# Layer 0 of a four-layer trunk: q's norm moved into the softmax's exponential, and the first shift weights loaded ahead of x

## The chip, the cores and the metric

One core of a Trainium2 chip runs the whole program in one launch. The metric is device time in microseconds, the median of three runs. The engines are TensorE (PE; PEld is its weight load), VectorE (DVE), ScalarE (ACT), GpSimd (POOL) and SyncE (SP), which issues nearly all transfers.

## The reference

Four layers of a diffusion transformer on 512 latent tokens and 256 context tokens of width 1024, in float32. Each layer normalizes its input, scales and shifts it by numbers made from a conditioning vector, mixes tokens (layer 0 by grouped attention) and ends with an MLP. The change lies in layer 0:

```python
def rms_norm(x, g):
    y = xf * lax.rsqrt(jnp.mean(xf * xf, axis=-1, keepdims=True) + EPS)
    return (y * g.astype(jnp.float32)).astype(x.dtype)
...
m = jax.nn.silu(vec) @ w + b          # ada_mods: shift, scale, gate, ...
hl = modulate(rms_norm(x, norm1_g[i]), ml[0], ml[1])      # h * (1.0 + scale) + shift
...
ql = apply_rope(rms_norm(ql.reshape(B, S, AT_HEADS, HEAD_DIM), q_g), ang) * scale
kl = apply_rope(rms_norm(kl.reshape(B, S, AT_KV_HEADS, HEAD_DIM), k_g), ang)
...
s = jnp.einsum('bqkgd,bnkd->bkgqn', q, k, preferred_element_type=jnp.float32)
p = jax.nn.softmax(s, axis=-1).astype(v.dtype)
```

There are 16 heads of q and 4 of k and v, each 64 wide. The norm of q is one number per token and head, so it is the same factor for a whole row of scores.

## The kernel before

Activations are held transposed, 128 channels on the partitions and tokens along the free axis. Every float32 matrix product is made of three products of a high and a low part (`mm3`, L124, L125, L127); ScalarE makes the high part and VectorE or GpSimd the low one (`split`, L104 and L105).

`start` (from L322) loads `x` in four transfers, puts the conditioning columns into rows (`sb`), and sums the squares of x: ScalarE squares one channel block (L345, L348), VectorE adds it (L349). `rstd` makes the reciprocal root, and the factor is spread over the partitions (`Rs`, L352 and L353). Scales come from VectorE's dot products of weight rows with `sb` (L223). The shift comes from TensorE: `sload(i)` loads half of its weights as four tiles `sw` (a ring of seven), `shift(i)` multiplies them with the conditioning columns (L389), ScalarE copies the row (L391), TensorE turns it into columns (L393), VectorE adds the bias (L394). There are two halves; the first is needed by the first four channel blocks. Then for each of eight blocks `modulate` makes h (VectorE L179, ScalarE L181, VectorE L182), and TensorE adds its share to k and v for three groups of 256 tokens.

`l0a` norms and rotates k, then makes q: four groups `g` of four heads, each for three token blocks `tp` (0 and 1 latent, 2 context), which gives twelve units in PSUM tiles of the role `mm` (four banks). Two units at a time go through `qk_norm` (ScalarE squares, L490; VectorE sums by head, L491; `rstd`) and `qk_unit`: VectorE multiplies by the norm (L499), GpSimd makes the sine part (L511) and VectorE the cosine part (L512), or for context the gain alone (L515); the result is split, transposed and written to DRAM (`qd`). Between the units `pump` gives VectorE dot products for the later scales. The last two units (`late`) are finished inside the attention.

`l0b` is the attention: 8 pairs of heads, 3 token blocks, 2 heads, 2 halves `u` of 128 tokens, so 96 times `front`. TensorE makes the scores into one of two PSUM tiles `s`, which take the banks of `mm` (L612); VectorE takes the negated row maximum (L614); ScalarE makes the exponential with it as its bias and sums the row (L616); TensorE transposes it (L621), ScalarE and VectorE split the copies (`pt`), and `back` multiplies with v (L635) and divides by the sums.

The order of each engine's instructions is set by the framework's scheduler, not by the code's order, except where an instruction is kept in place by `keep_in_program_order` (all loads of `load` among them).

Of the kernel before, what the change touches and what calls it, by code (L numbers as in the profile page):

```python
# [9 lines left out]
F = mybir.dt.float32  # L10
# [39 lines left out]
class Trunk:  # L50
# [78 lines left out]
    def rstd(self, ss, n, role="n", pin=False):  # L129
# [9 lines left out]
        last = ve.scalar_tensor_tensor(out=y, in0=v, scalar=1.5, in1=y, op0=ALU.add, op1=ALU.mult)  # L139
        if pin:  # L140
            self.tc.keep_in_program_order(last)
        return y
# [179 lines left out]
    def start(self):  # L322
# [4 lines left out]
        self.x = self.xp.tile([P, KC, TALL], F, name="x")  # L327
        for q in range(4):
            self.load(self.x[:, 2 * q:2 * q + 2], io["xT"][:, 2 * q:2 * q + 2])
# [5 lines left out]
        for v in range(2):  # L335
            for hf in range(2):
# [3 lines left out]
                nc.scalar.copy(out=self.sb[:, v, hf * 512:hf * 512 + 512], in_=rows)  # L340
        parts = parts_of(TALL)
# [13 lines left out]
        self.h0p = self.open("h0", "right")  # L355
        self.h = h = [self.h0p.tile([P, 2, TALL], R, name=f"h0_{j}") for j in range(KC)]
        self.kv_ps = [[self.ps("st" if w and tp == 2 else "pv" if tp == 2 else "mm") for tp in range(3)] for w in (1, 0)][::-1]
        al, ex = self.mod0
        st = self.open("start", "right")
# [18 lines left out]
        sws = {}  # L378

        def sload(i):  # L380
            for k in range(0, KC, 2):
                sws[i, k // 2] = st.tile([P, 2, 512], F, tag="sw", name="sw", bufs=7)
                self.load(sws[i, k // 2], io["ada_shift"][i][:, k:k + 2])

        def shift(i):

            rows, colv = self.ps("st"), self.ps("st")
            for k in range(KC):
                nc.tensor.matmul(rows[:2], sc[:, 2 * k:2 * k + 2], sws[i, k // 2][:, k % 2], start=(k == 0), stop=(k == KC - 1))  # L389
            r = st.tile([P, 512], F, tag="row", name="row", bufs=1)  # L390
            nc.scalar.copy(out=r[:2], in_=rows[:2])  # L391
            for n in range(4):
                nc.tensor.transpose(colv[:, 2 * n:2 * n + 2], r[:2, n * P:n * P + P], self.ident[:2, :2])  # L393
            nc.vector.tensor_tensor(out=al[:, 4 * i:4 * i + 4], in0=colv[:, :8].rearrange("p (n v) -> p n v", v=2),  # L394
                                    in1=self.vec("ada_b", 4 * i, 4 * i + 4).unsqueeze(2).to_broadcast([P, 4, 2]), op=ALU.add)

        self.share = 1 << 30
        self.pump_q = self.ada_work(0, (2, 3))
        sload(0)
# [4 lines left out]
        shift(0)  # L404
# [24 lines left out]
    def l0a(self):  # L429
# [3 lines left out]
        self.vp = kv.tile([P, 6, 4, 2, HD], R, name="vp")  # L433
        self.qd = self.dram.tile([8, P, 2, TALL], F, name="qd")
# [26 lines left out]
        for g in range(4):  # L461
            W = self.weight(io["wqkv0"][2 + g], self.wide, 256, 2)
            for tp in range(3):
# [7 lines left out]
                if len(wait) == 2 and (g, tp) != (3, 2):  # L471
                    finish()
# [885 lines left out]
```

## Time and profile before

| | us |
|---|---|
| median of 3 runs | 2752.83 |
| lowest and highest | 2746.94, 2753.98 |
| the profiled execution | 2748.76 |
| its span | 2747.0 |

Busy over the whole span: TensorE 2638.0 us (96%), VectorE 1776.1 us (65%), ScalarE 1154.8 us (42%), GpSimd 405.4 us (15%). Matrix products overlap and their ends are modelled, so TensorE's busy share says little of how near it is to its peak. These are averages over stages that differ; what follows is read stage by stage, from the span's start: `start` and the projections up to about 172 us, the hand-over, the attention up to 384 us, and all that comes behind.

### The profile page before, as it was taken

How to read it: one execution, taken by the hardware profiler on the slowest of the kernel's cores; microseconds unless marked ns; L12 is line 12 of the kernel's file. 1: busy time of each engine (PE TensorE's matmuls, PEld its weight loads, DVE VectorE, ACT ScalarE, POOL GpSimd, SP SyncE). 2: the span in 40 equal slices, each digit the busy share in tenths (PEclk: the TensorE clock that was granted, in tenths of full speed). 3: DMA queues.
4: the chain of work that ended last, by engine and by line, in shares of the span. 5: the costliest groups of instructions: out<-in, count | busy, mean ns of one | idle time of the engine just before them, and what ended most of it. 6: DMA issues, size and time to landing. Idle time of an engine off the chain costs nothing.

```text
span 2747.0 us, 39895 instructions
## 1 busy us (share of the span) xinstructions
PE 2638.0 (96%) x15472; PEld 2316.5 (84%) x15472; DVE 1776.1 (65%) x2827; ACT 1154.8 (42%) x2052; POOL 405.4 (15%) x359
## 2 busy tenths in 40 slices
PE   7989899999999999998999999998999998999998
PEld 5878778888888888988988889888888887988888
DVE  7988879766453372268766657998666657644445
ACT  3458864212121342268523335656322245533323
POOL 2321212000000030034200004543000012200002
PEclk8999999999999999999999999999999999999999
DMA  7431234445442256488466644213466633333334
GB/s 269 133 123 36 77 120 147 139 145 153 137 140 85 77 168 209 138 201 190 161 206 207 190 147 139 77 47 107 133 212 200 206 124 107 123 115 94 98 100 123
DMA packets 124844, 384.85 MB, mean 140 GB/s; under 512 B 17264, under 2 KB 37872, under 8 KB 123632
## 3 DMA queue, kind: packets, MB, share of 16 engines
q1 hardware_dynamic: 121392, 379.17, 44.2%
q10 hardware_dynamic: 3264, 3.15, 0.3%
q8 instruction: 122, 2.00, 0.3%
q14 instruction: 66, 0.54, 0.1%
HBM read 354.98 MB, written 27.26 MB: 139 GB/s over the span
## 4 chain that ended last, share of the span: by engine, by line
PE 49%; DVE 4%; DMA 2%; ACT 1%; issue 0%; POOL 0%; DVEq 0%; SPq 0%; ACTq 0%; POOLq 0%
PE ps_mm L124 15%; PE ps_mm L125 15%; PE ps_mm L127 15%; DVE ps_st L1162 1%; DMA k<-k 1%; DMA q<-q 1%; PE ps_cv L124 1%; PE ps_cv L125 1%; PE ps_cv L127 1%; DVE h L182 0%; PE ps_s L881 0%; PE ps_pt L890 0%; PE ps_cv L995 0%; PE ps_cv L998 0%; PE ps_cv L999 0%
## 5 line engine op out<-in xcount | busy, mean ns | idle before, releaser
L104 ACT CAST wh<-raw 128x1024 fp32r<-128x1024 f32 (+1 forms) x397 | 419.6, 1060 | 1030.6 <-PE ps_mm L125 606.5
L105 DVE TENSOR_TENSOR wl<-raw,wh 128x1024 fp32r<-128x1024 f32 (+1 forms) x368 | 463.7, 1262 | 372.6 <-ACT wh L104 369.5
L194 POOL TENSOR_TENSOR S<-S,tmp_q 128x256 f32<-128x256 f32 (+1 forms) x104 | 144.8, 1392 | 1684.8 <-ACT tmp_q L193 1680.7
L124 PE MATMUL ps_mm<-u,wh 128*128 128x512 f32 (+1 forms) x1088 | 374.9, 346 | 0.0
L125 PE MATMUL ps_mm<-u,wh 128*128 128x512 f32 (+1 forms) x1088 | 373.8, 345 | 0.0
L127 PE MATMUL ps_mm<-u,wl 128*128 128x512 f32 (+1 forms) x1088 | 373.6, 346 | 0.0
L125 PE MATMUL ps_mm<-hm,wh 128*128 128x512 f32 (+1 forms) x912 | 331.2, 365 | 0.0
L127 PE MATMUL ps_mm<-hm,wl 128*128 128x512 f32 (+1 forms) x912 | 331.0, 365 | 0.0
L124 PE MATMUL ps_mm<-hm,wh 128*128 128x512 f32 (+1 forms) x912 | 328.2, 366 | 1.1 <-ACT hm L181 1.1
L223 DVE CUSTOM_DVE_ANT_0 prod<-araw,sb 128x1024 bf16<-128x1024 f32 x224 | 276.4, 1234 | 6.5 <-DMA araw<-in_ada 5.3
L206 DVE SCALAR_TENSOR_TENSOR x<-ps_mm,mod,x 128x256 f32<-128x256 f32 (+1 forms) x192 | 115.1, 605 | 246.8 <-PE ps_mm L127 241.1
L125 PEld LDWEIGHTS ps_mm<-u,wh 128*128 128x128 f32 x1088 | 206.1, 189 | 25.0
L127 PEld LDWEIGHTS ps_mm<-u,wl 128*128 128x128 f32 x1088 | 205.9, 189 | 25.2
L124 PEld LDWEIGHTS ps_mm<-u,wh 128*128 128x128 f32 x1088 | 205.7, 189 | 25.3 <-DVE x L206 0.4
L127 PEld LDWEIGHTS ps_mm<-hm,wl 128*128 128x128 f32 x912 | 172.6, 189 | 27.6 <-DVE wl L105 0.4
L125 PEld LDWEIGHTS ps_mm<-hm,wh 128*128 128x128 f32 x912 | 172.7, 190 | 27.2
L124 PEld LDWEIGHTS ps_mm<-hm,wh 128*128 128x128 f32 x912 | 170.8, 190 | 28.7 <-ACT hm L181 1.5
L104 ACT CAST u<-tmp_r 128x512 fp32r<-128x512 f32 (+2 forms) x143 | 89.0, 624 | 171.1 <-DVE tmp_r L738 170.9
L124 PE MATMUL ps_big<-hm,wh 128*128 128x512 f32 x464 | 157.4, 339 | 0.8 <-ACT wh L104 0.8
L105 DVE TENSOR_TENSOR u<-tmp_r,u 128x512 fp32r<-128x512 f32 (+2 forms) x143 | 99.1, 695 | 86.6 <-ACT u L104 86.2
L125 PE MATMUL ps_big<-hm,wh 128*128 128x512 f32 x464 | 145.9, 337 | 0.0
L124 PE MATMUL ps_mm<-wh,h 128*128 128x256 f32 x448 | 129.9, 291 | 7.3 <-DVE tmp_r L499 2.9
(311 smaller groups left out, 5781.6 us busy)
## 6 DMA issues: line engine op xcount, KB each, us to landing
raw<-in_w SPq DMA_DIRECT2D x288, 512.0 KB, 3.9
araw<-in_ada SPq DMA_DIRECT2D x176, 512.0 KB, 3.7
raw<-in_wo SPq DMA_DIRECT2D x32, 512.0 KB, 4.3
raw<-in_wpw SPq DMA_DIRECT2D x24, 512.0 KB, 3.5
raw<-in_wqk SPq DMA_DIRECT2D x16, 512.0 KB, 4.1
q<-q SPq DMA_DIRECT2D x32, 256.0 KB, 9.1
raw<-in_wft SPq DMA_DIRECT2D x16, 512.0 KB, 3.8
k<-k SPq DMA_DIRECT2D x32, 224.0 KB, 9.4
```

Source lines behind the costliest of these rows:

```text
L104: self.nc.scalar.copy(out=H, in_=src)
L105: (low or self.nc.vector).tensor_tensor(out=L, in0=src, in1=H.bitcast(F), op=ALU.subtract)
L124: mm(o, lhs[0], rh, start=(k == 0), stop=False)
L125: mm(o, lhs[0], rl, start=False, stop=False)
L127: mm(o, lhs[1], rh, start=False, stop=last)
L194: (add or nc.gpsimd).tensor_tensor(out=S[:, :w], in0=S[:, :w], in1=q, op=ALU.add)
L206: self.nc.vector.scalar_tensor_tensor(out=xm, in0=self.like(ps), scalar=gate[:, m:m + 1], in1=xm, op0=ALU.mult, op1=ALU.add)
L223: ins = self.nc.vector.tensor_tensor_reduce(out=junk, in0=t, in1=self.sb[:, v], op0=ALU.mult, op1=ALU.add, scale=1.0, scalar=0.0, accum_ou ...
L1162: keep(nc.vector.scalar_tensor_tensor(out=y if last else a, in0=ut, scalar=wt, in1=a, op0=ALU.mult, op1=ALU.add))
```

## The change

**The start.** The first half of the shift's weights is loaded ahead of x, and its products, row copy and columns are written ahead of the sum of squares. The second half stays where it was.

```diff
         self.x = self.xp.tile([P, KC, TALL], F, name="x")
+        self.h0p = self.open("h0", "right")
+        st = self.open("start", "right")
...
+        sload(0)
         for q in range(4):
             self.load(self.x[:, 2 * q:2 * q + 2], io["xT"][:, 2 * q:2 * q + 2])
...
                 nc.scalar.copy(out=self.sb[:, v, hf * 512:hf * 512 + 512], in_=rows)
...
+        shift(0)
         parts = parts_of(TALL)
...
         self.pump_q = self.ada_work(0, (2, 3))
-        sload(0)
         for j in range(2):
             mods(j)
             wload(j)
         sload(1)
-        shift(0)
```

**The norm of q.** `squares` replaces the first half of `qk_norm`. A unit of q is no longer multiplied by its norm: for latent tokens ScalarE copies it out of PSUM for GpSimd, and VectorE's cosine product reads PSUM; for context the gain product reads PSUM. Units go through one at a time, and the norm is made once for the three units of a group, into `rsq`. In the attention the negated maximum is multiplied by the norm's column, and the exponential takes that column as its scale. k is treated as before, its three squares being summed by `squares` too.

```diff
+        self.rsq = kv.tile([P, 4, 24], F, name="rsq")
...
-            for a, r in zip(wait, self.qk_norm([a[0] for a in wait])):
-                self.qk_unit(a[0], r, a[1], 0, a[2], wk, tab, qkg)
+            for ps, tp, g in wait:
+                if tp == 0:
+                    sums[g] = self.small(24, "h")
+                self.squares(ps, sums[g], tp)
+                self.qk_unit(ps, None, tp, 0, g, wk, tab, qkg)
+                if tp == 2:
+                    self.rstd(sums[g], HD, "h", out=self.rsq[:, g])
                 self.pump(1)
...
-                if len(wait) == 2 and (g, tp) != (3, 2):
+                if g < 3 or tp == 0:
                     finish()
...
-        qn = self.tmp("r")
-        nc.vector.tensor_tensor(out=qn.rearrange("p (n d) -> p n d", d=HD), in0=ps.rearrange("p (n d) -> p n d", d=HD),
-                                in1=rs.unsqueeze(2).to_broadcast([P, 8, HD]), op=ALU.mult)
+        if rs is not None:
+            qn = self.tmp("r")
+            nc.vector.tensor_tensor(out=qn.rearrange("p (n d) -> p n d", d=HD), in0=ps.rearrange("p (n d) -> p n d", d=HD),
+                                    in1=rs.unsqueeze(2).to_broadcast([P, 8, HD]), op=ALU.mult)
+        elif tp < 2:
+            qn = self.tmp("r")
+            nc.scalar.copy(out=qn[:, :512], in_=ps)
+        else:
+            qn = ps
+        qn = qn[:, :512]
...
-            nc.vector.tensor_tensor(out=o4, in0=q4, in1=tab[:, a, 0, 2 * tp:2 * tp + 2].unsqueeze(2).to_broadcast([P, 2, 4, HD]), op=ALU.mult)
+            c4 = q4 if rs is not None else ps.rearrange("p (t h d) -> p t h d", t=2, h=4)
+            nc.vector.tensor_tensor(out=o4, in0=c4, in1=tab[:, a, 0, 2 * tp:2 * tp + 2].unsqueeze(2).to_broadcast([P, 2, 4, HD]), op=ALU.mult)
...
             nc.vector.tensor_reduce(out=mx, in_=ps[:, kc:TALL], axis=AX.X, op=ALU.max, negate=True)
+            n = part * 8 + u * 4 + pair % 2 * 2 + hh
+            rs = self.rsq[:, pair // 2, n:n + 1]
+            nc.vector.tensor_tensor(out=mx, in0=mx, in1=rs, op=ALU.mult)
             p = wk.tile([P, TALL], F, tag="p", name="p", bufs=3)
-            nc.scalar.activation(p[:, kc:], ps[:, kc:TALL], AF.Exp, bias=mx, accum_out=sums[:, u, hh:hh + 1])
+            nc.scalar.activation(p[:, kc:], ps[:, kc:TALL], AF.Exp, bias=mx, scale=rs, accum_out=sums[:, u, hh:hh + 1])
```

The scheduler lays the instructions out anew. Line numbers in the order of the change are its own; `small`, `tmp` and `mod` are the norm's columns, the work tiles and the scales and shifts. TensorE at the start, before (L339 the conditioning rows, L155 and L148 the sum over channels and its spread, L389 and L393 the shift, L124 the first products):

```order
L339 MATMUL ps_st<-ident,scol 128x128 x16
L155 MATMUL ps_st<-ones,tmp_r 128x1 x6
L148 MATMUL ps_st<-ident,small_ny 128x128 x6
L389 MATMUL ps_st<-sw,scol 2x512 x8
L393 MATMUL ps_st<-ident,row 128x2 x4
L124 MATMUL ps_mm<-wh,h_0_187 128x256
```

and in the changed kernel:

```order
L350 MATMUL ps_st<-ident,scol 128x128 x16
L358 MATMUL ps_st<-sw,scol 2x512 x8
L362 MATMUL ps_st<-ident,row 128x2 x4
L156 MATMUL ps_st<-ones,tmp_r 128x1 x6
L149 MATMUL ps_st<-ident,small_ny 128x128 x6
L124 MATMUL ps_mm<-wh,h_0_215 128x256
```

VectorE at the same place, before (L349 the additions of squares, L135 to L137 the norm's chain):

```order
L334 TENSOR_TENSOR scol<-scol,vecs 128x16
L349 TENSOR_TENSOR tmp_r<-tmp_r,araw 128x768 x7
L135 TENSOR_SCALAR small_nv<-ps_st 128x6
L136 RECIPROCAL small_ny<-small_nr 128x6
L137 TENSOR_TENSOR small_nv<-small_nv,small_ny 128x6
```

and in the changed kernel:

```order
L345 TENSOR_TENSOR scol<-scol,vecs 128x16
L375 TENSOR_TENSOR tmp_r<-tmp_r,araw 128x768 x3
L363 TENSOR_TENSOR mod_69<-ps_st,vecs 128x8
L375 TENSOR_TENSOR tmp_r<-tmp_r,araw 128x768 x4
L135 TENSOR_SCALAR small_nv<-ps_st 128x6
```

The shift's products and columns have moved ahead of the sum over channels on TensorE, and its bias addition (L394, now L363) to between the third and the fourth addition of squares on VectorE, where before it stood just ahead of the first low part of h (L182).

VectorE at the end of the projections, before, from the last sums of squares (L491) to the first maximum (L614):

```order
L491 TENSOR_REDUCE small_h<-tmp_q 128x8
L105 TENSOR_TENSOR pk<-S,pk 128x8x64 x2
L491 TENSOR_REDUCE small_h<-tmp_q 128x8
L135 TENSOR_SCALAR small_hv<-small_h 128x16
L136 RECIPROCAL small_hy<-small_hr 128x16
L137 TENSOR_TENSOR small_hv<-small_hv,small_hy 128x16
L138 TENSOR_TENSOR small_hv<-small_hv,small_hy 128x16
L139 SCALAR_TENSOR_TENSOR small_hy<-small_hv,small_hy 128x16
L499 TENSOR_TENSOR tmp_r<-ps_mm,small_hy 128x512 x2
L512 TENSOR_TENSOR S<-tmp_r,tab 128x512
L515 TENSOR_TENSOR S<-tmp_r,qkg 128x512
L614 TENSOR_REDUCE small_m<-ps_s 128x1 x2
```

and in the changed kernel, where L498 is the sum, L526 and L529 the table products, L628 the maximum and L631 the new multiplication:

```order
L498 TENSOR_REDUCE small_h<-tmp_q 128x8
L526 TENSOR_TENSOR S<-ps_mm,tab 128x512
L105 TENSOR_TENSOR pk<-S,pk 128x8x64
L498 TENSOR_REDUCE small_h<-tmp_q 128x8
L529 TENSOR_TENSOR S<-ps_mm,qkg 128x512
L135 TENSOR_SCALAR small_hv<-small_h 128x24
L136 RECIPROCAL small_hy<-small_hr 128x24
L137 TENSOR_TENSOR small_hv<-small_hv,small_hy 128x24
L138 TENSOR_TENSOR small_hv<-small_hv,small_hy 128x24
L105 TENSOR_TENSOR pk<-S,pk 128x8x64
L140 SCALAR_TENSOR_TENSOR rsq<-small_hv,small_hy 128x24
L628 TENSOR_REDUCE small_m<-ps_s 128x1 x2
```

The table products stand directly behind the sums of squares and read PSUM; the norm's chain (L135 to L140) comes behind them.

VectorE within the attention, before, a stretch of one pair of heads (L614 maximum, L105 low part of the transposed exponential, L568 fold, L555 and L557 the reciprocal of the row sums):

```order
L614 TENSOR_REDUCE small_m<-ps_s 128x1
L105 TENSOR_TENSOR pt_3578<-ps_st,pt_3577 128x384
L614 TENSOR_REDUCE small_m<-ps_s 128x1
L105 TENSOR_TENSOR pt_3578<-ps_st,pt_3577 128x384
L105 TENSOR_TENSOR pt_3636<-ps_st,pt_3635 128x256
L555 RECIPROCAL rs<-sums 128x4
L557 COPY tmp_q<-rs 128x256
L105 TENSOR_TENSOR pt_3636<-ps_st,pt_3635 128x256
L614 TENSOR_REDUCE small_m<-ps_s 128x1
L568 TENSOR_TENSOR tmp_t<-ps_pv,tmp_t 64x256
L614 TENSOR_REDUCE small_m<-ps_s 128x1
L568 TENSOR_TENSOR tmp_t<-ps_pv,tmp_t 64x256
```

and in the changed kernel (L628 maximum, L631 the new multiplication, L582 fold):

```order
L628 TENSOR_REDUCE small_m<-ps_s 128x1
L105 TENSOR_TENSOR pt_3403<-ps_st,pt_3402 128x384
L631 TENSOR_TENSOR small_m<-small_m,rsq 128x1
L582 TENSOR_TENSOR tmp_t<-ps_pv,tmp_t 64x256
L105 TENSOR_TENSOR pt_3403<-ps_st,pt_3402 128x384 x2
L628 TENSOR_REDUCE small_m<-ps_s 128x1
L631 TENSOR_TENSOR small_m<-small_m,rsq 128x1
L105 TENSOR_TENSOR pt_3470<-ps_st,pt_3469 128x384
L628 TENSOR_REDUCE small_m<-ps_s 128x1
L569 RECIPROCAL rs<-sums 128x4
L631 TENSOR_TENSOR small_m<-small_m,rsq 128x1
L571 COPY tmp_q<-rs 128x256
```

Some of the multiplications stand directly behind their maximum, others one or more instructions later. On SyncE's queue, behind the attention, two loads of scale weights (`araw`) have also moved ahead of the second load of x.

## Rows read from the trace of the kernel before

**Rows 1.** Stages of layer 0: busy us by engine, granted clock, DMA.
```profile
core 0: us, PE busy (x) PEld busy (x) DVE busy (x) ACT busy (x) POOL busy (x), PEclk, DMA share, GB/s
34.00:84.00 50.00, 45.60 (x314) 38.28 (x315) 48.78 (x89) 19.94 (x36) 9.53 (x10) 0.95 0.49 169
84.00:172.00 88.00, 83.60 (x665) 82.28 (x665) 86.18 (x144) 35.18 (x62) 33.91 (x26) 0.95 0.49 162
172.00:185.00 13.00, 6.72 (x45) 5.74 (x44) 7.90 (x15) 5.72 (x10) 5.17 (x5) 0.87 0.25 81
185.00:384.00 199.00, 179.40 (x1269) 158.77 (x1270) 172.06 (x351) 172.86 (x453) 37.74 (x47) 0.97 0.14 46
```

**Rows 2.** VectorE's timeline: start, us, instruction [idle before, releaser].
```profile
9.80 6.27 DVE L349 TENSOR_TENSOR tmp_r<-tmp_r,araw 128x768 f32<-128x768 f32 x6 [1.24 <-ACT araw L348]
...
33.42 0.17 DVE L394 TENSOR_TENSOR mod<-ps_st,vecs 128x8 f32<-128x8 f32 x1 [4.86 <-PE ps_st L393]
34.38 1.15 DVE L182 SCALAR_TENSOR_TENSOR h<-tmp_t,mod,h 128x512 fp32r<-128x512 f32 x2 [0.79 <-ACT h L181]
```

**Rows 3.** Timelines of TensorE and ScalarE, the shift's products and the cast.
```profile
22.54 8.01 PE L389 MATMUL ps_st<-sw,scol 128*2 128x512 f32 x16
...
31.48 0.40 ACT L375 CAST wh<-raw 128x256 fp32r<-128x256 f32 x1 [7.79 <-DMA raw<-in_wqkv]
```

**Rows 4.** X's transfers (first and last issue), SyncE's timeline.
```profile
L100 SPq DMA_DIRECT2D x<-in_xT x4: 417/428/477, 1.2 to 2.6; - x4
DMA to landing us min/median/max: 4.7/6.9/9.0
...
15.44 10.32 SPq L100 DMA_DIRECT2D sw<-in_ada_shift  x4
```

**Rows 5.** Stretches of the start, columns as in rows 1.
```profile
8.00:10.00 2.00, 0.00 (x0) 0.00 (x0) 0.77 (x2) 2.00 (x5) 0.00 (x0) 1.00 1.02 427
...
22.00:24.00 2.00, 2.00 (x5) 0.42 (x4) 1.89 (x6) 1.47 (x4) 0.53 (x1) 0.50 0.94 373
26.00:28.00 2.00, 2.00 (x6) 0.42 (x5) 2.00 (x4) 0.00 (x0) 0.00 (x0) 1.00 0.68 209
```

**Rows 6.** Lines L499 and L512 (ns min/median/max), and VectorE's timeline of one norm.
```profile
L499 DVE TENSOR_TENSOR tmp_r<-ps_mm,small_hy x14: 679/682/692, 94.3 to 180.6; 128x512 f32<-128x512 f32 x14
...
L512 DVE TENSOR_TENSOR S<-tmp_r,tab x10: 680/1220/1234, 96.9 to 181.2; 128x512 f32<-128x512 f32 x10
...
167.43 0.17 DVE L135 TENSOR_SCALAR small_hv<-small_h 128x16 f32<-128x16 f32 x1
...
168.41 1.29 DVE L499 TENSOR_TENSOR tmp_r<-ps_mm,small_hy 128x512 f32<-128x512 f32 x2
```

**Rows 7.** Timelines of ScalarE, TensorE and VectorE at the hand-over to attention.
```profile
176.03 0.60 ACT L490 ACTIVATE tmp_q<-ps_mm 128x512 f32<-128x512 f32 x1 [0.62 <-PE ps_mm L127]
...
180.78 2.29 PE L612 MATMUL ps_s<-kd,q 128*128 128x512 f32 x8 [4.35 <-DVE tmp_r L499]
...
183.16 1.81 DVE L614 TENSOR_REDUCE small_m<-ps_s 128x1 f32<-128x768 f32 x2
```

**Rows 8.** Two pairs of heads (columns as in rows 1); VectorE's timeline.
```profile
251.44:275.11 23.67, 21.84 (x159) 19.34 (x159) 21.40 (x45) 21.05 (x57) 4.44 (x6) 1.00 0.10 34
...
322.41:350.18 27.77, 24.31 (x158) 21.79 (x159) 22.93 (x46) 23.21 (x56) 9.05 (x8) 0.88 0.42 143
...
252.81 0.17 DVE L555 RECIPROCAL rs<-sums 128x4 f32<-128x4 f32 x1
252.90 0.53 DVE L105 TENSOR_TENSOR pt<-ps_st,pt 128x384 fp32r<-128x384 f32 x1
...
256.89 0.18 DVE L555 RECIPROCAL rs<-sums 128x4 f32<-128x4 f32 x1
257.10 0.29 DVE L557 COPY tmp_q<-rs 128x256 f32<-128x256 f32 x1
```

**Rows 9.** VectorE's timeline behind attention.
```profile
391.88 0.75 DVE L206 SCALAR_TENSOR_TENSOR x<-ps_mm,mod,x 128x512 f32<-128x512 f32 x1 [5.50 <-DMA x<-in_xT]
```

More of the change, by code (lines that the diff above doesn't have):

```diff
@@ L327, in start, with sload @@
         self.x = self.xp.tile([P, KC, TALL], F, name="x")
+        self.h0p = self.open("h0", "right")
+        st = self.open("start", "right")
+        sws = {}
+        def sload(i):
+            for k in range(0, KC, 2):
+                sws[i, k // 2] = st.tile([P, 2, 512], F, tag="sw", name="sw", bufs=7)
+                self.load(sws[i, k // 2], io["ada_shift"][i][:, k:k + 2])
+        sload(0)
         for q in range(4):
@@ L340, in start, with shift @@
                 nc.scalar.copy(out=self.sb[:, v, hf * 512:hf * 512 + 512], in_=rows)
+        al, ex = self.mod0
+        def shift(i):
+            rows, colv = self.ps("st"), self.ps("st")
+            for k in range(KC):
+                nc.tensor.matmul(rows[:2], sc[:, 2 * k:2 * k + 2], sws[i, k // 2][:, k % 2], start=(k == 0), stop=(k == KC - 1))
+            r = st.tile([P, 512], F, tag="row", name="row", bufs=1)
+            nc.scalar.copy(out=r[:2], in_=rows[:2])
+            for n in range(4):
+                nc.tensor.transpose(colv[:, 2 * n:2 * n + 2], r[:2, n * P:n * P + P], self.ident[:2, :2])
+            nc.vector.tensor_tensor(out=al[:, 4 * i:4 * i + 4], in0=colv[:, :8].rearrange("p (n v) -> p n v", v=2),
+                                    in1=self.vec("ada_b", 4 * i, 4 * i + 4).unsqueeze(2).to_broadcast([P, 4, 2]), op=ALU.add)
+        shift(0)
         parts = parts_of(TALL)
@@ L376, in wload @@
                 nc.gpsimd.tensor_tensor(out=L[:, j], in0=raw[:, j], in1=H[:, j].bitcast(F), op=ALU.subtract)
[L378 to L395, printed above, removed]
         self.share = 1 << 30
         self.pump_q = self.ada_work(0, (2, 3))
-        sload(0)
         for j in range(2):
@@ L448, in l0a @@
             self.split(pv, *(self.vp[:, 2 * tp:2 * tp + 2, :, s] for s in range(2)))
[L449 removed]
+        ss = self.small(24, "h")
         for tp in range(3):
[L451 removed]
+            self.squares(self.kv_ps[0][tp], ss, tp)
+        rs = self.rstd(ss, HD, "h")
+        for tp in range(3):
+            self.qk_unit(self.kv_ps[0][tp], rs[:, 8 * tp:8 * tp + 8], tp, 1, 0, wk, tab, qkg)
             self.pump(1)
[L453 removed]
+        wait, sums = [], {}
         def finish():
[L456 to L457 removed]
+            for ps, tp, g in wait:
[5 more added lines that the diff above has]
+                    self.rstd(sums[g], HD, "h", out=self.rsq[:, g])
                 self.pump(1)
```

27 lines of the change are left out of this document (8 added, 19 removed).

## The prediction

> **What bounds the kernel now.** The change touches only layer 0, so I first cut its span into stages and read each engine's busy time there [rows 1]. From 34 to 172 us, in the front projections, VectorE is the bound: 48.78 of 50 us and then 86.18 of 88 us busy, with TensorE behind it. From 172 to 185 us, where projections give way to attention, nobody works much: 6.72 us of TensorE and 7.90 us of VectorE in 13. From 185 to 384 us, in attention, three engines are close together: TensorE 179.40, ScalarE 172.86 and VectorE 172.06 us of 199. So one microsecond of VectorE is worth about one microsecond before 172 us, nothing by itself in the hand-over, and something between nothing and one in attention. After 384 us only a few instructions change places.
>
> Second, the waits at the start. VectorE finishes the sum of squares at 16.07 us (9.80 + 6.27), and later stands still for 4.86 us until the shift is there (L394, at 33.42 us) and for 0.79 us until L182 [rows 2]. The shift is late because TensorE runs its products only from 22.54 to 30.55 us, and ScalarE, which must copy their row, stands in a cast that waits 7.79 us for a weight load [rows 3]. That load was held by SyncE: the second set of shift weights occupies its queue for 10.32 us, since the seven `sw` buffers are not free before the first products are done [rows 4].
>
> **The change, part by part.** *A, the start.* The four shift transfers (2.1 MB) now stand ahead of x in SyncE's queue. The last part of x was issued at 2.6 us and landed 9.0 us later, at 11.6 us [rows 4]; at 427 GB/s [rows 5] 2.1 MB take 4.9 us, so it lands near 16.5. The order adds a second thread: L394 stands between the third and the fourth of the seven additions, and behind it come four at 1.05 us each (6.27 / 6). TensorE's shift products (eight, in the trace sixteen instructions) take 8.01 us where part of them ran at half clock [rows 3]; they can start when the transposes ahead of them end near 8 us, so they end near 15 to 16 us, copy and column transposes end near 16.3 us, and four additions later the sum is there at 20.4 us. The transfer's own bound (16.5 us plus three steps, 19.6 us) is close to it. The sum is 4.3 us later than 16.07 us. From there to where VectorE now falls idle, at 28.56 us (33.42 - 4.86), the work is the same, so that point comes at 32.9 us; but the shift is there, and L182 follows at once instead of at 34.38 us. Gain: 1.5 us, not the 5.65 us that the two waits show. Bounds: if the sum is only 2 us late, 3.8 us are gained. If the products run wholly at half clock (the granted clock was 0.50 from 22 to 24 us after TensorE had been idle, 1.00 from 26 to 28 us [rows 5]), they last nearly 14 us, the sum is near 26.5 us and 5 us are lost. I take the first, since TensorE comes to these products from the transposes, at granted clock 1.00 still at 8 to 10 us. SyncE's 10.32 us vanish as well, but the loads that were behind them have no waiter left that sets the end.
>
> *B, projections up to 172 us.* For q the multiplication by the norm (L499) falls away: 12 instructions, ten of them before 172 us, at 0.6 us from start to start (1.29 us for two, less their overlap) [rows 6]: 6.0 us. The norm's chain of six instructions ran for each pair of units, six times; now once for each group, four times. Back to back its VectorE part took 0.98 us (167.43 to 168.41 us) [rows 6], threaded between other work about half; two fewer are 1 us. Added is a ScalarE copy for eight units, 0.6 us each like the square of the same tile [rows 7]: 4.8 us on an engine with 35.18 of 88 us busy [rows 1], hidden. VectorE is the bound, so the gain is 7 us. Bounds: TensorE has only 4.4 us of gaps there (88 - 83.60), so 4 us if its busy time is real work; and 11 us, if the eight L512 that now read PSUM run like L499, whose 14 never took over 0.692 us, and not at their median of 1.22 us [rows 6] (8 x 0.54 = 4.3 us).
>
> *C, the hand-over.* The last unit's square starts at 176.03 us, but the scores' first product waits until 180.78 us, 4.35 us of it on L499, which had to wait for the norm; the first maximum starts at 183.16 us [rows 7]. By the new order the scores' PSUM is free after square, copy and the two table multiplications, none of which needs the norm: about 1.9 us after 176.03 us, so near 178 us. The first maximum comes near 179.5 us, the first exponential behind two maxima and two new multiplications. I take 3 us, between 2 and 4.5.
>
> *D, attention.* 96 multiplications of 128x1 are added on VectorE, between each maximum and its exponential. No row shows one; the nearest is the reciprocal of 128x4. With an independent instruction behind it, it costs 0.09 us from start to start (252.81 to 252.90 us), with a dependent one 0.21 us (256.89 to 257.10 us) [rows 8]. In the new order 30 of the 96 stand right behind their maximum and 66 have one to four instructions between. The first kind I price at 0.22 us, the second at 0.09 us: 6.6 + 5.9 = 12.5 us of VectorE. A pair of heads takes 23.67 us, of which VectorE is busy 21.40 us [rows 8]. The idle 2.27 us could absorb it; but in the pair from 322.41 us, into which three weight splits fall, the period grew to 27.77 us although VectorE stood idle for 4.84 us of it [rows 8]: in this stage added work lengthens the period while every engine still has gaps. I let a fifth be absorbed: loss 10 us, period 24.9 us. Bounds: 2 us, if VectorE's gaps take nearly all; 20.2 us, if each costs 0.21 us and nothing is absorbed. ScalarE's exponential takes its scale from a column; as with its bias column I count nothing for that.
>
> By a rule of the Trainium skill ("VectorE: DVE Perf Modes", The DRAIN you can't avoid) the next VectorE instruction does not start until the pipe is empty, semaphore or not. The row of 0.17 us with the next start after 0.09 us does not agree. By the rule every one of the 96 would cost its full length wherever it stands, and the sum would be the first rival's, +8.7 us.
>
> *E, behind attention.* SyncE's order puts two transfers of 512 KB ahead of x's second load, for which VectorE waits 5.50 us at 391.88 us [rows 9]. They are 2.5 us at 427 GB/s, but VectorE can work on them meanwhile. Nothing, 2 us either way.
>
> The sum: -1.5 - 7 - 3 + 10 + 0 = **-1.5 us**, against the profiled execution's 2748.76 us: 2747.3 us. The median of the runs shown lies 4.1 us higher, at 2752.83 us, and would become 2751.3 us. I state 2750 us, between the two.
>
> **The rivals.** *Attention pays in full (slower).* The multiplication sits where three engines are tied together: two score buffers are held from product to exponential, and two thirds of the multiplications wait behind another VectorE instruction, so the exponential comes later, ScalarE's queue with it, then TensorE's transposes. At 0.21 us each and nothing absorbed attention loses 20.2 us: 20.2 - 11.5 = +8.7 us, 2761.5 us on the median, and up to 2767 us with the delay on top. It decides when a pair takes over 26.2 us (8 x 2.5 = 20). For it: the gaps did not absorb the weight splits. Against: 66 of 96 cost less than half of that by the row. Chance 0.19.
>
> *Attention absorbs it (faster).* VectorE's gaps take the small instructions; D is 2 us, the sum -9.5 us, and with L512 faster too -13.8 us: 2743 to 2739 us. It decides when a pair takes under 24.1 us. For it: 2.27 us idle against 1.6 us added in a pair; against it the same pair from 322.41 us. Chance 0.24.
>
> *The start turns round.* The change puts x behind the shift, and the norm behind both: if the products run at half clock, the sum ends near 26.5 us and the early shift does not do what it is there for. A becomes +5 us, the sum +5 us: 2758 us, inside what can be told from no change. Chance 0.07.
>
> **How the numbers follow.** The forecast case (a pair of 24.1 to 26.2 us, sum between -8 and +8 us) has 0.50. Within 0.3%, which is 8.3 us and about what a measurement of this kernel can tell from no change, lie the forecast and the turned start: 0.57. Faster by more: 0.24; slower by more: 0.19. The bounds added up reach from about -20 to +21 us, which would need every term at its end; leaving out 2 in 10 gives -16 to +13 us on the median: 2737 to 2766 us.
>
> **What would show it.** In the profile of the changed kernel L394 should start near 16 us, the last addition end near 20.4 us, and L182 follow without a wait near 33 us; the end of the projections should come 8 to 9 us earlier, the first score product about 11 us earlier, near 170 us; a pair of heads should take 24.9 us, with the small multiplications at 0.17 us each. Wrong would be: additions that end after 24 us; projections no shorter, with TensorE or ScalarE busy all through; or a pair under 24.1 or over 26.2 us.

## The result and the profile after

The changed kernel takes **2787.2 us** (median of four runs, 2785.8 to 2789.5) against 2749.9 us of the kernel before beside it: a ratio of **1.0136, 95% interval 1.0116 to 1.0156**. It is 37 us slower; the forecast was 2750 us, with a range up to 2766 us.

The profiled execution spans 2784.0 us, 37.0 us more than before. Cut at three places it shows where they are:

| | before | after | difference |
|---|---|---|---|
| first score product of attention starts | 180.78 | 177.04 | -3.7 |
| from there to the first product of `wo0` | 203.6 | 243.5 | **+39.9** |
| from there to the end of the span | 2362.6 | 2363.4 | +0.8 |

The loss is in attention and nowhere else (`wo0` is the attention's output weight, whose products come right behind it). The stages, with the columns of [rows 1], which they answer:

```profile
34.00:84.00 50.00, 43.74 (x305) 36.64 (x304) 48.90 (x91) 18.42 (x32) 8.83 (x9) 0.94 0.49 168
84.00:168.00 84.00, 77.27 (x621) 75.73 (x620) 77.50 (x120) 37.53 (x67) 37.45 (x27) 0.96 0.50 169
168.00:181.00 13.00, 10.84 (x86) 10.28 (x84) 5.72 (x13) 4.96 (x10) 2.78 (x4) 1.00 0.23 81
181.00:421.00 240.00, 190.39 (x1274) 164.70 (x1275) 188.83 (x447) 187.95 (x454) 39.50 (x48) 0.96 0.12 40
```

In attention VectorE works 16.8 us and ScalarE 15.1 us more than in the last line of [rows 1], in a stage that is 41 us longer; no engine is busy for more than 80% of it, where three were at 86 to 90%. So no engine has become the bound; the engines wait for each other. One pair of heads of the steady part, after (it answers the first line of [rows 8]):

```profile
262.76:289.90 27.14, 22.61 (x158) 19.71 (x158) 23.92 (x57) 22.75 (x57) 4.44 (x6) 1.00 0.08 30
```

27.14 us against 23.67, at a granted TensorE clock of 1.00 in both: VectorE is idle for 3.2 us of it, ScalarE for 4.4, TensorE for 4.5. Whom TensorE waits for in attention stands in its list of waits (us in total, times, the longest), here the first line of before and the first two of after:

```profile
PE ps_st L621 <- ACT p L616: 6.2, 12, 2.1
```

```profile
PE ps_st L638 <- ACT p L633: 29.2, 31, 5.0
PE ps_pv L652 <- DVE pt L105: 10.3, 18, 1.5
```

The transposes of the probabilities (L621, now L638) stand in TensorE's queue and wait for the exponential 29.2 us instead of 6.2; what is behind them in the queue waits too. And the exponential waits for the new multiplication. ScalarE's first and third wait in attention before, then its first two after:

```profile
ACT pt L104 <- PE ps_st L621: 14.3, 22, 2.1
...
ACT p L616 <- DVE small_m L614: 4.1, 2, 3.8
```

```profile
ACT pt L104 <- PE ps_st L638: 22.7, 37, 1.4
ACT p L633 <- DVE small_m L631: 18.0, 34, 1.5
```

One front (product, maximum, multiplication, exponential) of the steady part, from the timeline of all engines (start, us, engine and line, operation):

```profile
301.13 0.94 DVE L628 TENSOR_REDUCE small_m<-ps_s 128x1 f32<-128x768 f32 x1
...
302.00 0.55 DVE L105 TENSOR_TENSOR pt<-ps_st,pt 128x384 fp32r<-128x384 f32 x1
...
302.46 0.15 DVE L631 TENSOR_TENSOR small_m<-small_m,rsq 128x1 f32<-128x1 f32 x1
...
303.11 1.01 ACT L633 ACTIVATE p<-ps_s,small_m,rsq 128x768 f32<-128x768 f32 x1
```

The maximum ends at 302.07. VectorE then does a low part of the front before (L105), and only at 302.46 the multiplication, whose own 0.15 us are the smallest item; meanwhile, at 302.37, ScalarE has begun two casts of transposes (L104), and the exponential starts 1.04 us behind the maximum. I call this stretch, from the end of a maximum to the start of its exponential, the **gap**. Taken over all 96 fronts (nth maximum with nth exponential) its mean is 0.68 us before and 1.35 us after: 0.70 us until the multiplication starts, 0.25 us for it, 0.40 us from its end to the exponential.

### The profile page after: what moved, and what is told of

The parts are those of the page before. It is cut to its first block, busy times and chain, and to the rows that moved or that the text cites. A ratio compares the mean times of both kernels' runs of the same rounds, so it can differ in the third digit from the quotient of the medians.

```text
span 2784.0 us, 40011 instructions
## 1 busy us (share of the span) xinstructions
PE 2649.4 (95%) x15472; PEld 2324.6 (83%) x15472; DVE 1782.3 (64%) x2901; ACT 1171.9 (42%) x2058; POOL 408.2 (15%) x359
## 4 chain that ended last, share of the span: by engine, by line
PE 78%; DVE 11%; DMA 5%; ACT 3%; issue 2%; POOL 0%; SPq 0%; DVEq 0%; ACTq 0%; POOLq 0%
PE ps_mm L124 18%; PE ps_mm L125 18%; PE ps_mm L127 18%; PE ps_big L124 6%; PE ps_big L127 6%; PE ps_big L125 6%; DMA k<-k 2%; DVE small_m L628 2%; DVE pt L105 2%; ACT p L633 1%; DVE prod L224 1%; DVE ps_st L1179 1%; DMA qd<-qs 1%; PE ps_pv L652 1%; PE ps_st L638 1%
## 5 line engine op out<-in xcount | busy, mean ns | idle before, releaser
L104 ACT CAST wh<-raw 128x1024 fp32r<-128x1024 f32 (+1 forms) x397 | 419.5, 1060 | 1036.2 <-PE ps_mm L125 601.7
L105 DVE TENSOR_TENSOR wl<-raw,wh 128x1024 fp32r<-128x1024 f32 (+1 forms) x368 | 465.0, 1265 | 376.1 <-ACT wh L104 373.4
L124 PE MATMUL ps_mm<-u,wh 128*128 128x512 f32 (+1 forms) x1088 | 374.9, 346 | 0.0
L124 PE MATMUL ps_mm<-hm,wh 128*128 128x512 f32 (+1 forms) x912 | 328.2, 366 | 1.1 <-ACT hm L182 1.1
L124 PEld LDWEIGHTS ps_mm<-u,wh 128*128 128x128 f32 x1088 | 205.7, 189 | 25.6 <-DVE x L207 0.4
L125 PEld LDWEIGHTS ps_mm<-u,wh 128*128 128x128 f32 x1088 | 206.1, 189 | 24.9
L125 PEld LDWEIGHTS ps_mm<-hm,wh 128*128 128x128 f32 x912 | 172.7, 190 | 27.1
L124 PEld LDWEIGHTS ps_mm<-hm,wh 128*128 128x128 f32 x912 | 170.8, 190 | 28.9 <-ACT hm L182 1.5
L104 ACT CAST u<-tmp_r 128x512 fp32r<-128x512 f32 (+2 forms) x143 | 89.0, 624 | 170.6 <-DVE tmp_r L755 170.3
L124 PE MATMUL ps_big<-hm,wh 128*128 128x512 f32 x464 | 157.4, 339 | 0.8 <-ACT wh L104 0.8
L105 DVE TENSOR_TENSOR u<-tmp_r,u 128x512 fp32r<-128x512 f32 (+2 forms) x143 | 99.0, 695 | 86.5 <-ACT u L104 86.2
L124 PE MATMUL ps_mm<-wh,h 128*128 128x256 f32 x448 | 130.1, 292 | 7.6 <-ACT h L182 4.6
```

The costliest lines, as they stand in the source:

```text
L104: self.nc.scalar.copy(out=H, in_=src)
L105: (low or self.nc.vector).tensor_tensor(out=L, in0=src, in1=H.bitcast(F), op=ALU.subtract)
L124: mm(o, lhs[0], rh, start=(k == 0), stop=False)
L125: mm(o, lhs[0], rl, start=False, stop=False)
```

## The experiments

First I took the change apart. Theory A1: the multiplication costs it; A2: the exponential's scale column; B: neither, but the new order of the work.

**no_factor**, the attention as before, the rest as changed:

```diff
-            nc.vector.tensor_tensor(out=mx, in0=mx, in1=rs, op=ALU.mult)
-            nc.scalar.activation(..., AF.Exp, bias=mx, scale=rs, ...)
+            nc.scalar.activation(..., AF.Exp, bias=mx, ...)
```

> The changed kernel with the factor taken out of the attention: no multiplication of the maximum, no scale column in the exponential; q stays without its norm (this part of the computation is left out). Theory A (the two additions in the attention cost all of it): the pair period goes back to 23.7 us, attention to about 204 us, and the time to 2746 us (2749.9 less the 3.7 us that the changed kernel has gained by the first score product). Theory B (the new order of the work from the projections on costs it, not the additions): the period stays over 26 us and the time over 2770 us.

Measured: 2750.9 us, 1.0002 (0.9993 to 1.0012); a pair takes 23.66 us, attention 206.1 us. With the factor out all of the loss is gone, so B falls, as far as the new order does not itself come from the factor. But the 3.7 us ahead of attention did not reach the median either.

**mult_only**, factor and scale as `self.one`, a column of ones; the exponential without `scale`:

```diff
+            nc.vector.tensor_tensor(out=mx, in0=mx, in1=self.one, op=ALU.mult)
+            nc.scalar.activation(..., AF.Exp, bias=mx, ...)
```

> The changed kernel with the multiplication of the maximum kept, by a column of ones, and the exponential without a scale column (q's norm is left out of the computation). Theory A1 (the multiplication in the chain from maximum to exponential carries most, 0.25 us on VectorE and a place further back in its queue): period about 26.5 us, time 2770 to 2783 us. Theory A2 (the exponential that is 0.09 us longer with a column carries most): period about 24 us, time below 2755 us.

Measured: 2803.3 us, 1.0192 (1.0176 to 1.0207), attention 253.9 us, gap 1.52 us. In attention the multiplication alone costs more than the whole change, 47.8 us over no_factor, and twice its own 23 us: a sum of durations does not give it. Its pairs are uneven, 26.7 to 33.2 us, where those of the changed kernel settle at 27.1; why it is slower than the whole change isn't settled.

**scale_only**, `scale=self.one` in the exponential, no multiplication:

> The changed kernel with a scale column of ones in the exponential and no multiplication of the maximum (q's norm is left out of the computation). Theory A1: 96 exponentials longer by 0.09 us, 8.6 us on ScalarE, a part of them hidden: 2750 to 2755 us, the rest of the loss gone with the multiplication. Theory A2: 2775 us or more. If each alone costs little (both below 2757 us), it is the two together that fill the slack of the loop.

Measured: 2753.4 us, 1.0011 (1.0001 to 1.0021), attention 207.9 us. The column costs its time on ScalarE, but hardly anything at the end. Line L630 of no_factor and L633 of this run (min/median/max ns):

```profile
L630 ACT ACTIVATE p<-ps_s,small_m x96: 474/902/943, 181.8 to 378.6; 128x768 f32<-128x768 f32 x64, 128x256 f32<-128x256 f32 x32
```

```profile
L633 ACT ACTIVATE p<-ps_s,small_m,one x96: 571/996/1027, 182.4 to 381.7; 128x768 f32<-128x768 f32 x64, 128x256 f32<-128x256 f32 x32
```

**start_only**, the shift's loads and products ahead of x, q's norm where it was:

> The kernel before with the first part of the change alone: the shift's weights and products ahead of x, q's norm where it was. Theory (the start gains, the attention loses): the 3.5 us by which the first part of h comes earlier in the changed kernel reach the end whole, 2746 us, and the pair period stays at 23.7 us. Rival (the projections take it back, since TensorE waits there for other work): 2749 to 2750 us.

Measured: 2758.9 us, 1.003 (1.002 to 1.004): neither. The first low part of h comes at 31.17 us, 3.2 us earlier than before, but the first score product only 0.6 us earlier (180.21), attention takes 208.4 us, and 6 us more than before pass behind it. There, from the first product of `wo0` to the end, the kernels run here differ by -5 to +11 us from the kernel before (2357.8 to 2373.6 us), in steps of some 2 to 4 us in layers that none of them edits. Why isn't settled; so below attention itself is compared, cut out of the trace, beside the time.

**q_only**, the second part of the change alone:

> The second part of the change alone: q's norm in the exponential's factor, the shift's weights where they were before. Theory (the attention loses and the start brings the 3.5 us that the trace of the changed kernel shows): 2788 to 2793 us, first score product near 180 us, period about 27 us. Rival (the two parts do harm only together, as the start moves the projections' work against the loads): below 2775 us.

Measured: 2785.8 us, 1.014 (1.0123 to 1.0157), period 27.13 us, gap 1.35 us. It is the whole loss. Its first score product starts at 175.51 us, earlier than with both parts together (177.04): the start's gain does not add to this one.

So it is the multiplication. Next: what about it? Q: its place behind other work in VectorE's queue; L: its collisions with GpSimd; T: VectorE's time as such.

**ts_mult**, the same multiplication with the factor as a per-row scalar:

```diff
-            nc.vector.tensor_tensor(out=mx, in0=mx, in1=rs, op=ALU.mult)
+            nc.vector.tensor_scalar(out=mx, in0=mx, scalar1=rs, scalar2=None, op0=ALU.mult)
```

> The changed kernel with the multiplication of the maximum written as tensor by per-row scalar, so that VectorE reads one tensor from SBUF and the factor as a scalar, not two tensors. In the changed kernel 28 multiplications that met a GpSimd operation took 0.49 us on average and ended with it, 65 that met none took 0.15 us. Theory L (an operation on two SBUF tensors can't run beside GpSimd's): all 96 take about 0.15 us, VectorE gains some 9 us, time about 2775 us. Rival (the place in the queue and the step in the chain cost it, not these 9 us): time within 4 us of 2787 us, whatever the durations do.

Measured: 2776.0 us, 1.0096 (1.0079 to 1.0113). The line of the multiplication in the changed kernel, then in this run:

```profile
L631 DVE TENSOR_TENSOR small_m<-small_m,rsq x96: 139/149/742, 182.3 to 417.8; 128x1 f32<-128x1 f32 x96
```

```profile
L631 DVE TENSOR_SCALAR small_m<-small_m,rsq x96: 183/205/217, 187.3 to 412.0; 128x1 f32<-128x1 f32 x96
```

The scalar form is slower in the median but never longer than 0.22 us, whether GpSimd runs or not. L's forecast of some 2775 us held, 11 of the 37 us, though not its 0.15 us: VectorE saved 3.9 us on the multiplications, and the gap fell to 1.15 us.

**act_mult**, the multiplication on ScalarE right ahead of its exponential:

```diff
+            nc.scalar.activation(mx, mx, AF.Copy, scale=rs)
```

> The changed kernel with the multiplication of the maximum on ScalarE, right ahead of its exponential, instead of on VectorE. VectorE's queue is then that of the kernel before, ScalarE has 96 operations more of about 0.2 us, 19 us in all. Theory Q (the multiplication's place behind other work in VectorE's queue holds the exponentials back): the waits of the exponentials shrink, period 24.5 to 25.5 us, 2760 to 2768 us. Rival (any operation more between maximum and exponential costs its own time on the loop, 0.2 us twelve times and more): period over 26 us, 2775 us or more.

Measured: 2779.5 us, 1.0112 (1.0096 to 1.0129); one takes 0.30 us, not 0.2; period 26.66 us, gap 1.11 us. Q's forecast is missed and its rival's (over 26 us, 2775 us or more) met: out of VectorE's queue it costs nearly as much. ScalarE is now busy 24.80 of 26.66 us, so this run mixes a longer gap with a fuller engine.

**pool_mult**, on GpSimd:

```diff
+            nc.gpsimd.tensor_tensor(out=mx, in0=mx, in1=rs, op=ALU.mult)
```

> The changed kernel with the multiplication of the maximum on GpSimd, which is busy for 39.5 of the attention's 240 us. Theory B (VectorE's busy time is what the loop lacks): VectorE has its old work, period about 24 us, 2755 us. Rival (the length of the chain from maximum to exponential is what counts): the way over GpSimd adds its latency and, at times, 0.74 us of an operation in front, period over 27 us, 2785 us or more.

Measured: 2763.7 us, 1.0055 (1.004 to 1.007); period 24.68 us, gap 0.76 us. Here the multiplication starts 0.13 us behind its maximum, since GpSimd is mostly free. The forecasts (2755 us for VectorE's relief, which is T, and 2785 us or more for the chain) are both missed, and two readings fit: VectorE is relieved (T), or the gap is short.

**fused_ts**, maximum and factor in one pass over the scores, written to p (`rs` holds the negated factor):

```diff
-            nc.vector.tensor_reduce(out=mx, in_=ps[:, kc:TALL], axis=AX.X, op=ALU.max, negate=True)
-            nc.vector.tensor_tensor(out=mx, in0=mx, in1=rs, op=ALU.mult)
+            nc.vector.tensor_scalar(out=p[:, kc:], in0=ps[:, kc:TALL], scalar1=rs, scalar2=3.0e38,
+                                    op0=ALU.mult, op1=ALU.min, accum_out=mx)
+            nc.scalar.activation(p[:, kc:], p[:, kc:], AF.Exp, bias=mx, scale=-1.0, ...)
```

> The changed kernel with maximum and multiplication in one pass of VectorE: scores times the negated factor from PSUM into p, with the smallest of the row as the accumulated result; the exponential then reads p from SBUF with a scale of -1 and that bias, without a scale column; four more operations of 128x24 negate the factor ahead of the attention. No operation of its own is left for the factor but a read of the accumulator (0.08 us at L902 of the changed kernel). Theory (the separate multiplication costs it): the pass takes about the 0.95 us of the maximum, the exponential about as long as now, period 23.7 to 24.5 us, time 2746 to 2758 us. Rival (the pass that writes 128x768 is longer or stands in GpSimd's way): a pass of 1.2 us or more, period over 26 us, 2770 us or more.

Measured: 2755.4 us, 1.0024 (1.0014 to 1.0033), gap 0.48 us, a pair in 24.2 to 24.3 us. The wide pass takes 1.01 us and its accumulator read 0.08, together 0.14 more than the maximum's 0.95; 32 us of the loss are gone:

```profile
L632 DVE TENSOR_SCALAR_CACHE_REDUCE p<-ps_s,rsq 128x768 f32<-128x768 f32 x64 | 64.7, 1012 | 7.5 <-PE ps_st L638 5.7 <-PE ps_s L627 0.9
...
L632 DVE DVE_READ_ACCUMULATOR p<-ps_s,rsq 128x1 f32 x96 | 7.9, 83 | 0.0
```

I then held T for the likelier theory, and three runs were to show it.

**off_chain**, no factor, but a multiplication whose result nobody reads:

```diff
+            nc.vector.tensor_tensor(out=self.small(1, "j"), in0=mx, in1=self.one, op=ALU.mult)
```

> The changed kernel without the factor (q's norm is left out of the computation), but with 96 multiplications of the maximum by a column of ones on VectorE whose result nobody reads: the same queue time as in the run that kept the multiplication alone, but no exponential waits for it. Theory T (VectorE's time is what the loop lacks; that run lost 52 us by 23 us of operations): most of the loss stays, 2775 us or more, period over 26 us. Rival (the step in the chain from maximum to exponential, and where it stands in the queue, costs it): time below 2760 us, period below 24.5 us.

Measured: 2759.7 us, 1.0042 (1.0027 to 1.0057); attention 204.8 us, gap 0.60 us; what is lost in time lies behind attention (2373.6 us, 11 more than before). **T falls.** The same 96 operations are in VectorE's queue as in mult_only (18 and 23 us), but no exponential waits for them, and attention is 49 us shorter. Attention of off_chain, then of mult_only:

```profile
177.00:382.00 205.00, 179.42 (x1284) 159.83 (x1283) 186.07 (x455) 176.78 (x456) 37.91 (x47) 0.98 0.13 45
```

```profile
178.00:432.00 254.00, 203.44 (x1283) 171.10 (x1282) 193.04 (x455) 182.90 (x456) 38.56 (x48) 0.95 0.11 36
```

VectorE, here the busiest engine, does its 186 us in 205 without harm. It had the room; what the loop had not was time between maximum and exponential.

**before_copy** and **fused_copy**, the 24 copies of the reciprocals (0.29 us each on VectorE, 0.40 on GpSimd) moved to GpSimd, in the kernel before and in fused_ts:

```diff
-        nc.vector.tensor_copy(out=re.rearrange(
+        (nc.gpsimd if w == 256 else nc.vector).tensor_copy(out=re.rearrange(
```

> The kernel before with the 24 copies of the reciprocals over 128x256 (L557, 0.29 us each, 6.9 us) on GpSimd, which is idle for 160 of the attention's 199 us. Theory T (what VectorE's queue holds goes whole into the loop): the period falls by up to 0.9 us (3 copies of 0.29) to 22.8 to 23.3 us and the time by 3 to 7 us, to 2743 to 2746 us, faster than both kernels. Rival (TensorE, at 21.84 of 23.67 us, and the chain decide): period 23.6 us, time within 2 us of the kernel before.

> The one-pass form of maximum and factor with the 24 copies of the reciprocals on GpSimd as well. The one-pass form took 2755.4 us at a mean pair period of some 24.3 us, VectorE's pass and accumulator read being 0.15 us longer than the maximum. Theory T: 7 us less on VectorE give back 3 to 7 us, 2748 to 2752 us, level with the kernel before. Rival (its loop is bound by TensorE's wait for the score buffers): 2755 us, unchanged.

Measured: before_copy 2751.9 us, 1.0014 (1.0005 to 1.0023), period 23.81 us: relief of VectorE brings nothing, against T once more. fused_copy 2748.5 us, 1.000 (0.999 to 1.0009): its gain of 7 us over fused_ts is what T gave as a number, but it is no proof of T: in the profiled executions 3.0 us are gained in attention (210.4 to 207.4 us, a pair in 24.0 us) and 8.1 us behind it, in layers that neither edits, while 2.9 us are lost ahead of it. It is the best form of the change, 39 us faster than the changed kernel. Level with the kernel before it is only by the part behind attention (4.8 us shorter); its attention is 3.8 us longer. No run beat both kernels.

Left open was whether the gap itself is the cause, since each kernel with a longer gap had also put work on VectorE or ScalarE. The last two runs lengthen it on GpSimd alone:

**pool_x2, pool_x4**, behind pool_mult's multiplication one and three more by ones:

```diff
             nc.gpsimd.tensor_tensor(out=mx, in0=mx, in1=rs, op=ALU.mult)
+            nc.gpsimd.tensor_tensor(out=mx, in0=mx, in1=self.one, op=ALU.mult)
```

> The multiplication of the maximum on GpSimd, followed there by one more by a column of ones: one operation of 0.19 us more in the chain from maximum to exponential, on an engine that is idle for most of the attention. With one operation the time was 2763.7 us, attention 216.1 us, and the maximum's end lay 0.76 us ahead of the exponential's start on average. Theory C (the length of this chain sets the loop; over the runs so far some 0.55 us of attention per front for each us of it): gap about 1.0 us, attention about 226 us, time about 2774 us. Rival Q (the queue time on VectorE or ScalarE sets it): no more work there, 2762 to 2766 us.

> The same with three operations by ones behind the multiplication on GpSimd, 0.57 us more in the chain and none on VectorE or ScalarE. Theory C: gap about 1.35 us, as in the changed kernel, attention 240 to 250 us, time about 2790 us. Rival Q: 2762 to 2770 us. If GpSimd itself became the bound (58 us more on 39.5 and 19 us in some 230 us), its share would show it; at half of the time it is not.

Measured: 2780.5 us, 1.0104 (1.0081 to 1.0127), gap 1.15, attention 229.7 us; and 2799.1 us, 1.0175 (1.0155 to 1.0194), gap 1.56, attention 255.4 us. Theory C holds in both, at more than its numbers. Attention of pool_x4, and TensorE's first wait in it:

```profile
181.00:430.00 249.00, 190.59 (x1264) 165.12 (x1264) 180.29 (x352) 187.10 (x449) 110.33 (x430) 0.96 0.11 37
```

```profile
PE ps_st L643 <- ACT p L638: 43.5, 41, 4.1
```

GpSimd is busy for 44% of the stage and VectorE does less than in the changed kernel; yet the stage is longer than there. The fourteen kernels with a maximum of its own, in order of the gap (us):

| kernel | gap | attention |
|---|---|---|
| off_chain | 0.60 | 204.8 |
| no_factor | 0.67 | 206.1 |
| before | 0.68 | 203.6 |
| start_only | 0.74 | 208.4 |
| pool_mult | 0.76 | 216.1 |
| scale_only | 0.77 | 207.9 |
| before_copy | 0.77 | 205.2 |
| act_mult | 1.11 | 231.6 |
| ts_mult | 1.15 | 233.7 |
| pool_x2 | 1.15 | 229.7 |
| after | 1.35 | 243.5 |
| q_only | 1.35 | 245.8 |
| mult_only | 1.52 | 253.9 |
| pool_x4 | 1.56 | 255.4 |

A straight line through them misses none by more than 6 us and rises by 57 us per microsecond of gap, 0.6 us for each of the 96 fronts, whichever engine makes the gap. (The one-pass forms, with a longer pass in place of the maximum, stand outside: fused_ts 0.48 and 210.4, fused_copy 0.53 and 207.4.)

No run holds one thing fixed: the scheduler laid out each of these kernels anew. One trait of TensorE's queue can be counted in the traces: how many later score products stand ahead of a front's transposes. In the kernel before there are two or three at 68 of the 96 fronts, in the changed kernel at 9, and a single one at 86; so its transposes wait for the exponential also because they come earlier in the queue. The kernels with gaps below 0.8 us have 1.5 to 2.0 such products on average, act_mult 1.3. In the six kernels ts_mult, pool_x2, after, q_only, mult_only and pool_x4 there are 1.1 to 1.2, and among these attention still rises from 230 to 255 us with a gap of 1.15 to 1.56 us, at 60 us per microsecond. So the gap counts by itself; how much of the step from the short gaps to the long ones is the new order's isn't separated. The gap, too, holds in part what the scheduler put between a maximum and its multiplication.

## Why the prediction was wrong, step by step

**D, attention: the failed step.** It said "6.6 + 5.9 = 12.5 us of VectorE", a fifth of it absorbed, loss 10 us, a pair in 24.9 us. Measured: 39.9 us and 27.14 us. In the terms of the sum, -1.5 - 7 - 3 + 10 + 0 became -3.5 for A, -0.2 for B and C together, +39.9 for D and +0.8 for E. Four things in D were off, the last by far the most.
- *The price of one.* Forecast 0.09 or 0.22 us; measured 0.25 us on average (23.7 us in all). Of those that the timeline shows singly 65 took 0.15 us and 28, which met a GpSimd operation, 0.49 us.
- *The count.* "30 of the 96 stand right behind their maximum" counted each from the nearest maximum in the row. Counted nth with nth, 10 do; 86 have one to five other VectorE operations between.
- *The exponential.* "I count nothing": it costs 0.09 us more with a scale column, 7.9 us of ScalarE. By scale_only some 2 us of that reach the end of attention (207.9 against 206.1), so this did little harm.
- *The measure.* The step added up time in VectorE's queue. off_chain shows that this time is nearly free in attention, and the pool runs show that the same delay costs as much on an engine that has room. What had to be priced was the gap: 0.67 us more for each front, by the line above 38 of the 39.9 us. The rival "attention pays in full" named this mechanism ("the exponential comes later, ScalarE's queue with it, then TensorE's transposes") and its point of decision, 26.2 us a pair, was passed; but it too priced the operation, at 0.21 us, and not the wait in front of it (0.70 us) and behind it (0.40 us). That is why the range ended at 2766 us.

That attention follows the gap at about 0.6 is shown. The traces also show why the rate is near a half. Each of the two score buffers is held from the start of its score product to the end of its exponential, 3.34 us on average before and 4.22 us after, and the next product into the same buffer starts 0.81 and 0.80 us behind that end. With 48 turns for each buffer, 0.87 us more a turn are 42 us, against the 39.9 measured. In all fourteen kernels of the table that pause lies between 0.77 and 0.87 us, so a longer hold was nowhere absorbed. A third buffer was not tried.

**A, the start: the path right, one term off, the gain not kept.** VectorE's timeline of the changed kernel, which answers [rows 2]:

```profile
16.34 0.16 DVE L363 TENSOR_TENSOR mod<-ps_st,vecs 128x8 f32<-128x8 f32 x1
16.52 4.14 DVE L375 TENSOR_TENSOR tmp_r<-tmp_r,araw 128x768 f32<-128x768 f32 x4
30.89 2.09 DVE L183 SCALAR_TENSOR_TENSOR h<-tmp_t,mod,h 128x512 fp32r<-128x512 f32 x2
```

Forecast were "near 16 us" and "near 20.4 us" for the bias and the last addition: 16.34 and 20.66. L183 (L182 before) came at 30.89 us, not near 33: 3.5 us gained instead of 1.5. The sum of squares was 4.6 us late, much as forecast (4.3); wrong was that behind it "the work is the same". From the norm's first instruction (L135) on, VectorE had 9.4 us of it before (19.19 to 28.56 us) and 7.0 us after (23.84 to 30.89 us): four operations were shorter, and a pair of small scale operations (L367, L368 before) came behind L183. So the bound of 3.8 us, meant for a sum only 2 us late, holds by luck. The turned start did not happen. But start_only kept 0.6 us of it up to attention, and q_only was faster there without it.

**B and C, projections and hand-over: mis-sized.** Forecast was the first score product "about 11 us earlier, near 170 us"; it came 3.7 us earlier. One detail was right: L526 (L512 before) reads PSUM in 0.68 us. The first maximum starts 2.6 us earlier, at 180.60 us, where the terms A to C together gave 11.5 us. Wrong was "VectorE is the bound, so the gain is 7 us". From the first low part of h to the first score product before (34.40 us) and after (30.90 us):

```profile
34.40:180.78 146.38, 133.63 (x1013) 124.58 (x1013) 138.67 (x241) 59.57 (x104) 45.16 (x37) 0.95 0.48 161
```

```profile
30.90:177.04 146.14, 133.15 (x1011) 123.56 (x1011) 132.17 (x219) 60.28 (x109) 52.16 (x42) 0.95 0.49 165
```

VectorE did 6.5 us less, as forecast; the stage kept its length, and TensorE its 133 us of products and 13 us of idle time. Its waits only changed their names. These stand first in its list, before from 34.4 to 181 us and after from 31 to 177 us:

```profile
PE ps_s L612 <- DVE tmp_r L499: 4.3, 1, 4.3
PE ps_mm L124 <- DVE tmp_r L499: 2.9, 2, 1.8
```

```profile
PE ps_st L541 <- DVE pk L105: 2.9, 3, 1.5
PE ps_st L541 <- ACT qs L543: 2.7, 1, 2.7
PE ps_mm L124 <- ACT wh L104: 2.5, 1, 2.5
```

The prediction had taken 4 us, TensorE's gaps, for the least gain of B; with both parts of the change B and C together brought 0.2 us. q_only had gained 5.3 us by its first score product. Why the two parts together gain less than q_only alone isn't settled.

**E, behind attention: right as a number, in part by luck.** 2362.6 and 2363.4 us. But at the first reciprocal of this part, 57 us behind the first product of `wo0`, the changed kernel had gained 4.3 us, and layers that it does not edit took them back; the experiments show too that this part varies by more than the 2 us that the step allowed.

## What to carry to other kernels

In a loop whose engines are all 85 to 90% busy and which hands a tile from engine to engine, price an operation that is put into the chain by the delay from its producer's end to its consumer's start, not by its own duration: the queue ahead of it and behind it counts as well, and here each microsecond of delay cost 0.6 us per turn. Where a scheduler orders the queues, part of that delay is the place it gives the operation, so read the order as well. A test for the chain is cheap: the same operation with its result unread. If a factor must go in, put it into a pass that is there already, as in fused_copy.

## What the chip showed unexpectedly

**VectorE waits for GpSimd, even for 128x1.** From the timeline of the changed kernel:

```profile
299.66 0.73 POOL L105 TENSOR_TENSOR o<-tmp_t,o 128x256 fp32r<-128x256 f32 x1 [1.56 <-ACT o L104]
299.67 0.74 DVE L631 TENSOR_TENSOR small_m<-small_m,rsq 128x1 f32<-128x1 f32 x1
...
304.55 0.73 POOL L587 TENSOR_TENSOR tmp_t<-tmp_t,tmp_r 128x256 f32<-128x256 f32 x1 [4.16 <-ACT tmp_r L575]
305.02 0.28 DVE L631 TENSOR_TENSOR small_m<-small_m,rsq 128x1 f32<-128x1 f32 x1
```

A multiplication of two SBUF tensors that starts 0.01 us behind a GpSimd operation takes 0.74 us, one that starts 0.47 us behind takes 0.28: both end with it. With the factor as a scalar (ts_mult) 26 that met one took 0.21 us, like the rest (0.20). The Trainium skill ("SBUF — State Buffer", SBUF: two separate sides) says that a VectorE operation with two SBUF inputs and a GpSimd operation that reads SBUF exclude each other for the whole instruction; the trace agrees. The prediction's price for the multiplication left this out.

**A per-row operand of ScalarE has a price.** The exponential's median went from 902 to 992 ns with the scale as a column (996 in scale_only). The Trainium skill ("ScalarE: Activation LUTs", What ACT_TABLE_LOAD costs) gives about 93 ns for each such operand; the rows agree.

**The smallest operations cost about the same anywhere but on ScalarE.** One 128x1 multiplication has a median of 0.15 us on VectorE from two tensors, 0.205 us with a scalar, 0.19 us on GpSimd, and 0.30 us on ScalarE.
